# Attention scores for eight batches of eight heads: pairs of adjacent heads in block-diagonal q weights, and a new order of rows in the loads

## The chip, the cores and the metric

The kernel runs on one core of one Trainium2 chip. The metric is the device time of one execution in microseconds (us), as the median of several runs; lower is better.

## The reference

```python
batch, heads, seq, dim = 8, 8, 512, 64        # q, k: float32

def reference(q, k):
    scale = 1.0 / np.sqrt(q.shape[-1])
    return (np.einsum('bhqd,bhkd->bhqk', q, k) * scale).astype(np.float32)
```

For each of the 64 pairs of batch and head, a 512 x 64 matrix q is multiplied with the transpose of a 512 x 64 matrix k, and the result, 512 x 512, is scaled by 1/8. The inputs are 16.8 MB together and the output is 67.1 MB, all float32.

## The kernel before

The batches are taken two at a time: a unit v is batches 2v and 2v+1, and there are four units. A contraction over dim = 64 fills only half of the 128 rows of TensorE's array, so the two batches of a unit lie side by side: rows 0 to 63 hold the first batch, rows 64 to 127 the second (index x in the code).

**Loading and casting** (`load_and_cast`). For each unit and each of k and q, two loads (L70), one per batch, bring 1 MB each into a buffer `xf` of 128 partitions by 2048 floats. The view `q_r = q.rearrange("b g (m j) d -> b (g m) (j d)", j=R)` has R = 32: partition p is head g = p // 16 and row group m = p % 16, and it holds 32 consecutive rows of 64 floats, 8 KB. The source of one load is thus 1 MB of consecutive memory. A cast (L75) to bfloat16 follows, into half x of the tile `xb`; for unit 0 the casts are on VectorE and ScalarE, for the others on GpSimd (POOL). Six `xf` buffers and three `xb` buffers rotate.

**Transposing** (`transpose`). TensorE transposes 128 x 128 pieces of `xb`, 32 for k (L86) and 32 for q (L93) per unit, eight to a PSUM tile `tp` (two buffers). VectorE copies k's tiles into `kT` (L88), ScalarE q's into `qT` (L95). Afterwards partitions are (x, d), and the rows of a head are reached by strides. Each unit has its own `kT` and `qT`.

**Scores** (`scores`). One call works on two heads (2n and 2n+1) of both batches. Query row 8u + i of a head is row u of the stationary operand for that i. For each i there are four matmuls of 64 x 64 weights by 512 columns (L109), one for each head h and batch x. Their `tile_position=(x * D, h * U)` puts them on the four quarters of the array. Two values of i make one PSUM tile `ps` per batch, 128 x 1024 floats. It is scaled and copied to the output buffer `o`, alternately by ScalarE (L57) and VectorE (L59). When a buffer's four parts are filled, one transfer of 2 MB (L117) writes it to consecutive memory. Four `o` buffers rotate, and a call uses two of them.

**Order.** All transfers are issued by SyncE (SP), from one queue in program order, so the 16 loads stand ahead of the 32 outputs. A tile framework schedules the instructions of each engine by priority in program order and inserts the semaphores. By hand, the transposes of unit 1 stand behind the first call of `scores`, those of units 2 and 3 behind the second, so all transposes are done early. The rest of the scores follows.

Of the kernel before, what the change touches and what calls it, by code (L numbers as in the profile page):

```python
# [1 line left out]

# [5 lines left out]


@with_exitstack  # L10
def kernel(
    ctx: ExitStack,
    tc: tile.TileContext,
    q: bass.AP,
    k: bass.AP,
    out: bass.AP,
):

    nc = tc.nc
    B, H, S, D = q.shape
    scale = 1.0 / (D ** 0.5)
    P = 128
    UNITS = B // 2
    G = H
    M = P // G
    R = S // M  # L30
    RO = 8
    U = S // RO
    JJ = R // RO
    IW = 8 // JJ

    f32 = mybir.dt.float32
    bf16 = mybir.dt.bfloat16

    q_r = q.rearrange("b g (m j) d -> b (g m) (j d)", j=R)
    k_r = k.rearrange("b g (m j) d -> b (g m) (j d)", j=R)  # L40
    out_r = out.rearrange("b (n h) (u i) k -> b n (h u) (i k)", h=2, i=RO)

    consts = ctx.enter_context(tc.tile_pool(name="consts", bufs=1))
    raw_pool = ctx.enter_context(tc.tile_pool(name="raw", bufs=6))
    bf_pool = ctx.enter_context(tc.tile_pool(name="bf", bufs=3))
    t_pool = ctx.enter_context(tc.tile_pool(name="t", bufs=UNITS))
    out_pool = ctx.enter_context(tc.tile_pool(name="out", bufs=4))
    tpsum_pool = ctx.enter_context(tc.tile_pool(name="tpsum", bufs=2, space=bass.MemoryType.PSUM))
    psum_pool = ctx.enter_context(tc.tile_pool(name="psum", bufs=3, space=bass.MemoryType.PSUM))

    identity = None
    n_evac = 0

    def evacuate(dst, src):
        nonlocal n_evac
        if n_evac % 2 == 0:
            nc.scalar.mul(out=dst, in_=src, mul=scale)  # L57
        else:
            nc.vector.tensor_scalar(out=dst, in0=src, scalar1=scale, scalar2=None,  # L59
                                    op0=mybir.AluOpType.mult)  # L60
        n_evac += 1

    def load_and_cast(v):

        both = []
        for src in (k_r, q_r):
            xb = bf_pool.tile([P, R, 2, D], bf16, name="xb")
            for x in range(2):
                xf = raw_pool.tile([P, R * D], f32, name="xf")
                nc.sync.dma_start(out=xf, in_=src[2 * v + x])  # L70
                if v > 0:
                    copy = nc.gpsimd.tensor_copy
                else:
                    copy = (nc.vector.tensor_copy, nc.scalar.copy)[x]
                copy(out=xb[:, :, x, :], in_=xf.rearrange("p (j d) -> p j d", j=R))  # L75
            both.append(xb)
        return both

    def transpose(kb, qb):

        kT = t_pool.tile([P, P, R], bf16, name="kT")
        qT = t_pool.tile([P, RO, P, JJ], bf16, name="qT")
        for j0 in range(0, R, 8):
            tp = tpsum_pool.tile([P, 8, P], bf16, name="tp")
            for j in range(8):
                nc.tensor.transpose(out=tp[:, j, :], identity=identity,  # L86
                                    in_=kb[:, j0 + j].rearrange("p x d -> p (x d)"))
            nc.vector.tensor_copy(out=kT[:, :, j0:j0 + 8], in_=tp.rearrange("d j p -> d p j"))  # L88
        for i0 in range(0, RO, IW):
            tp = tpsum_pool.tile([P, IW, JJ, P], bf16, name="tp")  # L90
            for i in range(IW):
                for jj in range(JJ):
                    nc.tensor.transpose(out=tp[:, i, jj, :], identity=identity,  # L93
                                        in_=qb[:, RO * jj + i0 + i].rearrange("p x d -> p (x d)"))
            nc.scalar.copy(out=qT[:, i0:i0 + IW], in_=tp.rearrange("d i jj p -> d i p jj"))  # L95
        return kT, qT

    def scores(v, n, kT, qT):

        kTh = kT.rearrange("d (g m) j -> d g (m j)", g=G)  # L100
        qTh = qT.rearrange("d i (g m) jj -> d i g (m jj)", g=G)
        os = [out_pool.tile([P, RO, S], f32, name="o") for _ in range(2)]
        for i in range(0, RO, 2):
            pss = [psum_pool.tile([P, 2, S], f32, name="ps") for _ in range(2)]
            for w in range(2):
                for h in range(2):
                    for x in range(2):
                        rows = slice(x * D, (x + 1) * D)
                        nc.tensor.matmul(out=pss[x][h * U:(h + 1) * U, w, :],  # L109
                                         lhsT=qTh[rows, i + w, 2 * n + h, :],  # L110
                                         rhs=kTh[rows, 2 * n + h, :],
                                         start=True, stop=True,
                                         tile_position=(x * D, h * U))
            for x in range(2):
                evacuate(os[x][:, i:i + 2, :], pss[x])
        for x in range(2):
            nc.sync.dma_start(out=out_r[2 * v + x, n], in_=os[x].rearrange("p i k -> p (i k)"))  # L117

    cast = [load_and_cast(0)]
    identity = consts.tile([P, P], dtype=bf16)  # L120
    make_identity(nc, identity)
    for v in range(1, UNITS):
        cast.append(load_and_cast(v))

    ts = [transpose(*cast[0])]
    scores(0, 0, *ts[0])
    ts.append(transpose(*cast[1]))
    scores(0, 1, *ts[0])
    ts.append(transpose(*cast[2]))
    ts.append(transpose(*cast[3]))  # L130
    for v in range(UNITS):
        for n in range(2 if v == 0 else 0, H // 2):
            scores(v, n, *ts[v])


# [1 line left out]
_INS = ['q', 'k']  # L137
_OUTS = [((8, 8, 512, 512), 'float32')]


# [23 lines left out]
```

## Time and profile before

| | |
|---|---|
| median of 3 runs | 204.52 us (204.51 to 207.3) |
| profiled execution, its own time | 204.67 us |
| span of its profile | 202.9 us |
| TensorE (matmuls) busy | 134.3 us (66%) |
| VectorE busy | 96.2 us (47%) |
| ScalarE busy | 84.1 us (41%) |
| GpSimd (POOL) busy | 23.4 us (12%) |
| share of the 16 DMA engines' time, main queue | 97.6% |
| chain of work that ended last: DMA | 61% of the span |

The span runs from the first to the last recorded instruction; the execution's own time has a little more around it. An engine's busy time is the sum of its instructions' durations. The line of 40 slices gives one digit per slice of 5.07 us, the busy share in tenths; the GB/s line gives what the DMA engines moved in each. In the list of groups a row gives the line of the code, the engine, the operation, its output and input tiles with their sizes, the count, the total busy time and the mean of one, and then the idle time just before these instructions with what ended most of it.

### The profile page before, as it was taken

What the parts mean: (1) busy time and instruction counts of PE and PEld (TensorE: products, weight loads), DVE (VectorE), ACT (ScalarE), POOL (GpSimd) and SP (SyncE); (2) the same over time, 40 slices, a digit from 0 to 9 for tenths busy, and PEclk for the clock granted to TensorE, in tenths of its full rate; (3) what the DMA queues carried; (4) which work ended last, traced back from release to release, by engine and by line L of the source; (5) the groups of instructions that cost most, each with busy time, mean ns of one, the idle gap of its engine ahead of it and who ended that gap; (6) DMA issues with size and microseconds to landing.
All of it is one profiled execution on the core that took longest, in us unless ns stands there. A gap on an engine that the chain in (4) does not pass through costs nothing.

```text
span 202.9 us, 1888 instructions
## 1 busy us (share of the span) xinstructions
PE 134.3 (66%) x768; PEld 40.9 (20%) x768; DVE 96.2 (47%) x82; ACT 84.1 (41%) x83; POOL 23.4 (12%) x18
## 2 busy tenths in 40 slices
PE   0079698666396968787878787877778696766000
PEld 0066245454021111120211021111111121110000
DVE  0292799935182726354453636271809090909000
ACT  2336849265725243443525252535352525252000
POOL 1007757753000000000000000000000000000000
PEclk9999999999755555555555555555555555555555
DMA  5999999999999999999999999999999999999991
GB/s 218 431 426 423 418 426 417 420 428 423 439 423 426 436 430 430 433 426 433 426 426 433 428 428 430 436 423 426 433 423 436 431 423 436 426 423 433 433 426 74
DMA packets 6921, 84.01 MB, mean 414 GB/s; under 512 B 768, under 2 KB 768, under 8 KB 768
## 3 DMA queue, kind: packets, MB, share of 16 engines
q1 hardware_dynamic: 6912, 83.89, 97.6%
q8 instruction: 6, 0.10, 0.2%
q14 instruction: 3, 0.02, 0.0%
HBM read 16.78 MB, written 67.11 MB: 413 GB/s over the span
## 4 chain that ended last, share of the span: by engine, by line
DMA 61%; DVE 12%; PE 8%; ACT 7%; SPq 2%; issue 1%; DVEq 0%
DMA out_dram<-o 57%; DVE o L59 9%; PE ps L109 6%; ACT o L57 5%; DMA xf<-in_q_dram 4%; DVE kT L88 2%; ACT qT L95 2%; PE tp L93 2%; SPq L117 1%; PE tp L86 1%; DVE xb L75 1%; SPq L70 0%; DVEq L59 0%
## 5 line engine op out<-in xcount | busy, mean ns | idle before, releaser
L109 PE MATMUL ps<-kT,qT 64*64 64x512 bf16 x512 | 113.5, 584 | 35.2 <-ACT o L57 29.5
L59 DVE TENSOR_SCALAR o<-ps 128x1024 f32<-128x1024 f32 x64 | 75.6, 1220 | 78.5 <-DMA out_dram<-o 72.8
L57 ACT ACTIVATE o<-ps 128x1024 f32<-128x1024 f32 x64 | 63.9, 1024 | 82.9 <-PE ps L109 82.8
L109 PEld LDWEIGHTS <-qT 64*64 64x64 bf16 x512 | 23.2, 127 | 120.4 <-issue 117.8
L75 POOL CAST xb<-xf 128x2048 bf16<-128x2048 f32 x12 | 22.7, 1895 | 23.2 <-DMA xf<-in_k_dram 18.1
L88 DVE COPY kT<-tp 128x1024 bf16<-128x1024 bf16 x16 | 18.7, 1216 | 3.4 <-PE tp L86 3.3
L86 PE MATMUL tp<-identity,xb 128*128 128x128 bf16 x128 | 11.3, 241 | 13.2 <-ACT xb L75 10.1
L95 ACT COPY qT<-tp 128x1024 bf16<-128x1024 bf16 x16 | 15.6, 1016 | 10.3 <-PE tp L93 10.1
L93 PE MATMUL tp<-identity,xb 128*128 128x128 bf16 x128 | 10.7, 235 | 3.5 <-DVE kT L88 1.7
L86 PEld LDWEIGHTS <-xb 128*128 128x128 bf16 x128 | 9.0, 108 | 17.1 <-ACT xb L75 10.1
L93 PEld LDWEIGHTS <-xb 128*128 128x128 bf16 x128 | 8.7, 105 | 6.9 <-issue 5.7
L75 ACT CAST xb<-xf 128x2048 bf16<-128x2048 f32 x2 | 3.8, 1897 | 9.2 <-DMA xf<-in_k_dram 6.1
L75 DVE CAST xb<-xf 128x2048 bf16<-128x2048 f32 x2 | 2.5, 1228 | 9.4 <-DMA xf<-in_k_dram 5.6
L75 ACT ACT_TABLE_LOAD x1 | 1.3, 1283 | 0.7 <-PEq L148 0.7
masks.py:199 POOL TENSOR_SCALAR_AFFINE_SELECT identity<-identity 128x128 bf16<-128x128 bf16 x1 | 0.3, 293 | 0.1
masks.py:197 POOL MEMSET identity<- 128x128 bf16 x1 | 0.2, 205 | 0.3 <-POOLq L148 0.3
L148 POOL MEMSET const-float32-0.0<- 128x1 f32 x1 | 0.1, 100 | 0.2 <-issue 0.2
L148 POOL MEMSET const-bfloat16-1.0<- 128x1 bf16 x1 | 0.1, 102 | 0.0
L148 POOL MEMSET const-uint8-127<- 128x1 uint8 x1 | 0.1, 102 | 0.0
L148 POOL MEMSET const-float32-1.0<- 128x1 f32 x1 | 0.1, 99 | 0.0
## 6 DMA issues: line engine op xcount, KB each, us to landing
out_dram<-o SPq DMA_DIRECT2D x32, 2048.0 KB, 14.4
xf<-in_k_dram SPq DMA_DIRECT2D x8, 1024.0 KB, 14.0
xf<-in_q_dram SPq DMA_DIRECT2D x8, 1024.0 KB, 13.7
```

The lines of the kernel that those rows point to most:

```text
L57: nc.scalar.mul(out=dst, in_=src, mul=scale)
L59: nc.vector.tensor_scalar(out=dst, in0=src, scalar1=scale, scalar2=None, op0=mybir.AluOpType.mult)
L75: copy(out=xb[:, :, x, :], in_=xf.rearrange("p (j d) -> p j d", j=R))
L86: nc.tensor.transpose(out=tp[:, j, :], identity=identity, in_=kb[:, j0 + j].rearrange("p x d -> p (x d)"))
L88: nc.vector.tensor_copy(out=kT[:, :, j0:j0 + 8], in_=tp.rearrange("d j p -> d p j"))
L93: nc.tensor.transpose(out=tp[:, i, jj, :], identity=identity, in_=qb[:, RO * jj + i0 + i].rearrange("p x d -> p (x d)"))
L95: nc.scalar.copy(out=qT[:, i0:i0 + IW], in_=tp.rearrange("d i jj p -> d i p jj"))
L109: nc.tensor.matmul(out=pss[x][h * U:(h + 1) * U, w, :], lhsT=qTh[rows, i + w, 2 * n + h, :], rhs=kTh[rows, 2 * n + h, :], start=True, stop ...
L117: nc.sync.dma_start(out=out_r[2 * v + x, n], in_=os[x].rearrange("p i k -> p (i k)"))
L148: nc = _bacc.Bacc("TRN2", target_bir_lowering=False, num_devices=1)
```

## The change

- **Units and halves.** A unit is still two batches, but the halves x are now the even and the odd heads: half x of pair (b, n) is head 2n + x of batch b. There are eight pairs c = (b, n) in a unit.
- **Loads.** One load takes all even or all odd heads of both batches: `src[v, x]` has 16 row groups m, then 8 pairs c, then 8 KB. Partition p is m = p // 8 and pair c = p % 8. The source of one load is 128 pieces of 8 KB. Two that follow one another in one row group m lie 256 KB apart.
- **Weights.** q is kept in two standing tiles `qz`, used in turn by the units. For each i and pair c, `qz` holds 128 x 128 weights: rows 0 to 63 and columns 0 to 63 are the even head's q, rows 64 to 127 and columns 64 to 127 the odd head's. The other two quarters are zero; `clear` (L82) writes them once at the start, one of the four by VectorE and three by GpSimd. Copies of q (L105) touch only the two filled quarters, one half on VectorE and the other on ScalarE.
- **Matmuls.** One matmul of 128 x 128 weights by 512 columns (L116) gives 64 query rows of both heads, so there are 256 in place of 512. An output buffer holds one pair of heads.
- **Copies of k** (L94) alternate between VectorE and ScalarE, and lay `kT` out by pair.
- **Order.** The transposes of unit v + 1 stand in the middle of the scores of unit v.
- **Buffers.** `xf` 6 to 4, `xb` 3 to 5, `kT` 4 to 2, `o` 4 to 5.

In the changed kernel the transposes are L91 and L100, and the output transfer is L120; L57, L59, L70 and L75 keep their numbers.

```diff
-    G = H
-    M = P // G
+    C = H
+    M = P // C
...
-    q_r = q.rearrange("b g (m j) d -> b (g m) (j d)", j=R)
-    k_r = k.rearrange("b g (m j) d -> b (g m) (j d)", j=R)
-    out_r = out.rearrange("b (n h) (u i) k -> b n (h u) (i k)", h=2, i=RO)
+    q_r = q.rearrange("(v b) (n x) (m j) d -> v x m (b n) (j d)", b=2, x=2, j=R)
+    k_r = k.rearrange("(v b) (n x) (m j) d -> v x m (b n) (j d)", b=2, x=2, j=R)
+    out_r = out.rearrange("(v b) (n x) (u i) k -> v (b n) (x u) (i k)", b=2, x=2, i=RO)
...
-    raw_pool = ctx.enter_context(tc.tile_pool(name="raw", bufs=6))
-    bf_pool = ctx.enter_context(tc.tile_pool(name="bf", bufs=3))
-    t_pool = ctx.enter_context(tc.tile_pool(name="t", bufs=UNITS))
-    out_pool = ctx.enter_context(tc.tile_pool(name="out", bufs=4))
+    raw_pool = ctx.enter_context(tc.tile_pool(name="raw", bufs=4))
+    bf_pool = ctx.enter_context(tc.tile_pool(name="bf", bufs=5))
+    t_pool = ctx.enter_context(tc.tile_pool(name="t", bufs=2))
+    out_pool = ctx.enter_context(tc.tile_pool(name="out", bufs=5))
...
-                nc.sync.dma_start(out=xf, in_=src[2 * v + x])
+                nc.sync.dma_start(out=xf, in_=src[v, x])
...
+    def clear(engine, qz, x):
+
+        rows = slice(x * D, (x + 1) * D)
+        engine.memset(qz[rows, :, :, (1 - x) * U:(2 - x) * U], 0.0)
+
+    def transpose(v, kb, qb):
...
-        kT = t_pool.tile([P, P, R], bf16, name="kT")
-        qT = t_pool.tile([P, RO, P, JJ], bf16, name="qT")
-        for j0 in range(0, R, 8):
+        kT = t_pool.tile([P, C, M, R], bf16, name="kT")
+        qz = qzs[v % 2]
+        for n, j0 in enumerate(range(0, R, 8)):
...
-            nc.vector.tensor_copy(out=kT[:, :, j0:j0 + 8], in_=tp.rearrange("d j p -> d p j"))
+            copy = (nc.vector.tensor_copy, nc.scalar.copy)[n % 2]
+            copy(out=kT[:, :, :, j0:j0 + 8].rearrange("d c m j -> d m c j"),
+                 in_=tp.rearrange("d j (m c) -> d m c j", c=C))
...
-            nc.scalar.copy(out=qT[:, i0:i0 + IW], in_=tp.rearrange("d i jj p -> d i p jj"))
-        return kT, qT
+            for x in range(2):
+                rows = slice(x * D, (x + 1) * D)
+                copy = (nc.vector.tensor_copy, nc.scalar.copy)[x]
+                copy(out=qz[rows, i0:i0 + IW, :, x * U:(x + 1) * U]
+                     .rearrange("d i c (m jj) -> d i c m jj", jj=JJ),
+                     in_=tp[rows].rearrange("d i jj (m c) -> d i c m jj", c=C))
+        return kT, qz
...
+                nc.tensor.matmul(out=ps[:, w, :], lhsT=qz[:, i + w, c, :],
+                                 rhs=kT[:, c].rearrange("d m j -> d (m j)"),
+                                 start=True, stop=True)
+            evacuate(o[:, i:i + 2, :], ps)
+        nc.sync.dma_start(out=out_r[v, c], in_=o.rearrange("p i k -> p (i k)"))
...
+    qzs = [consts.tile([P, RO, C, P], bf16, name=f"qz{n}") for n in range(2)]
+    clear(nc.vector, qzs[0], 0)
+    clear(nc.gpsimd, qzs[0], 1)
+    for x in range(2):
+        clear(nc.gpsimd, qzs[1], x)
...
-    ts = [transpose(*cast[0])]
-    scores(0, 0, *ts[0])
-    ts.append(transpose(*cast[1]))
-    scores(0, 1, *ts[0])
-    ts.append(transpose(*cast[2]))
-    ts.append(transpose(*cast[3]))
+    ts = {0: transpose(0, *cast[0])}
...
-        for n in range(2 if v == 0 else 0, H // 2):
-            scores(v, n, *ts[v])
+        for c in range(C):
+            scores(v, c, *ts[v])
+            if c == C // 2 - 1 and v + 1 < UNITS:
+                ts[v + 1] = transpose(v + 1, *cast[v + 1])
```

More of the change, by code (lines that the diff above doesn't have):

```diff
@@ L37 @@
     bf16 = mybir.dt.bfloat16
-    q_r = q.rearrange("b g (m j) d -> b (g m) (j d)", j=R)
-    k_r = k.rearrange("b g (m j) d -> b (g m) (j d)", j=R)
-    out_r = out.rearrange("b (n h) (u i) k -> b n (h u) (i k)", h=2, i=RO)
+    q_r = q.rearrange("(v b) (n x) (m j) d -> v x m (b n) (j d)", b=2, x=2, j=R)
+    k_r = k.rearrange("(v b) (n x) (m j) d -> v x m (b n) (j d)", b=2, x=2, j=R)
+    out_r = out.rearrange("(v b) (n x) (u i) k -> v (b n) (x u) (i k)", b=2, x=2, i=RO)
     consts = ctx.enter_context(tc.tile_pool(name="consts", bufs=1))
-    raw_pool = ctx.enter_context(tc.tile_pool(name="raw", bufs=6))
-    bf_pool = ctx.enter_context(tc.tile_pool(name="bf", bufs=3))
-    t_pool = ctx.enter_context(tc.tile_pool(name="t", bufs=UNITS))
-    out_pool = ctx.enter_context(tc.tile_pool(name="out", bufs=4))
+    raw_pool = ctx.enter_context(tc.tile_pool(name="raw", bufs=4))
+    bf_pool = ctx.enter_context(tc.tile_pool(name="bf", bufs=5))
+    t_pool = ctx.enter_context(tc.tile_pool(name="t", bufs=2))
+    out_pool = ctx.enter_context(tc.tile_pool(name="out", bufs=5))
     tpsum_pool = ctx.enter_context(tc.tile_pool(name="tpsum", bufs=2, space=bass.MemoryType.PSUM))
     psum_pool = ctx.enter_context(tc.tile_pool(name="psum", bufs=3, space=bass.MemoryType.PSUM))
-    identity = None
     n_evac = 0
@@ L77, in load_and_cast @@
         return both
-    def transpose(kb, qb):
-        kT = t_pool.tile([P, P, R], bf16, name="kT")
-        qT = t_pool.tile([P, RO, P, JJ], bf16, name="qT")
-        for j0 in range(0, R, 8):
+    def clear(engine, qz, x):
[5 more added lines that the diff above has]
+        for n, j0 in enumerate(range(0, R, 8)):
             tp = tpsum_pool.tile([P, 8, P], bf16, name="tp")
@@ L94, in transpose, with scores @@
                                         in_=qb[:, RO * jj + i0 + i].rearrange("p x d -> p (x d)"))
-            nc.scalar.copy(out=qT[:, i0:i0 + IW], in_=tp.rearrange("d i jj p -> d i p jj"))
-        return kT, qT
[L98 to L102, printed above, removed]
+            for x in range(2):
[5 more added lines that the diff above has]
+        return kT, qz
+    def scores(v, c, kT, qz):
+        o = out_pool.tile([P, RO, S], f32, name="o")
         for i in range(0, RO, 2):
-            pss = [psum_pool.tile([P, 2, S], f32, name="ps") for _ in range(2)]
+            ps = psum_pool.tile([P, 2, S], f32, name="ps")
             for w in range(2):
[L106 to L117, printed above, removed]
+                nc.tensor.matmul(out=ps[:, w, :], lhsT=qz[:, i + w, c, :],
[3 more added lines that the diff above has]
+        nc.sync.dma_start(out=out_r[v, c], in_=o.rearrange("p i k -> p (i k)"))
     cast = [load_and_cast(0)]
```

## The prediction

> **What bounds the kernel now.** I read the slices and the queue totals first, then the stages, then who waits at the outputs, then the load stage in order of time.
>
> ```profile
> DMA  5999999999999999999999999999999999999991
> GB/s 218 431 426 423 418 426 417 420 428 423 439 423 426 436 430 430 433 426 433 426 426 433 428 428 430 436 423 426 433 423 436 431 423 436 426 423 433 433 426 74
> ...
> q1 hardware_dynamic: 6912, 83.89, 97.6%
> ...
> HBM read 16.78 MB, written 67.11 MB: 413 GB/s over the span
> ```
>
> From the second slice to the last but one the 16 DMA engines are full, and no slice moves more than 439 GB/s. The stages say the same:
>
> ```profile
> core 0: us, PE busy (x) PEld busy (x) DVE busy (x) ACT busy (x) POOL busy (x), PEclk, DMA share, GB/s
> ...
> 3.00:43.00 40.00, 26.37 (x268) 16.63 (x269) 25.61 (x22) 22.26 (x22) 19.86 (x11) 1.00 1.01 423
> ...
> 60.00:180.00 120.00, 92.91 (x397) 18.55 (x392) 56.55 (x48) 49.48 (x50) 0.00 (x0) 0.50 1.01 429
> ```
>
> The first row is the loads, the second the outputs. Both have a DMA share of 1, at 423 and 429 GB/s. In the output stage TensorE runs at half clock and VectorE and ScalarE are under half busy. The waits of VectorE and the chain of waits confirm that compute waits for DMA:
>
> ```profile
> DVE o L59 <- DMA out_dram<-o: 72.8, 14, 6.8
> ...
> 69.84 14.39 DMA out_dram<-o
> ...
> 89.29 14.39 DMA out_dram<-o
> ```
>
> The chain repeats every 89.29 - 69.84 = 19.45 us, which is one turn of the four output buffers: 4 x 2.097 MB / 19.45 us = 431 GB/s, or 4.86 us an output. The load stage, by the casts, each of which starts when its load has landed:
>
> ```profile
> 5.62 1.23 DVE L75 CAST xb<-xf 128x2048 bf16<-128x2048 f32 x1 [5.62 <-DMA xf<-in_k_dram]
> ...
> 10.59 1.23 DVE L75 CAST xb<-xf 128x2048 bf16<-128x2048 f32 x1 [3.74 <-DMA xf<-in_q_dram]
> ...
> 15.59 1.89 POOL L75 CAST xb<-xf 128x2048 bf16<-128x2048 f32 x1 [14.28 <-DMA xf<-in_k_dram]
> ```
>
> Loads 0, 2 and 4 land 4.98 us apart: 2.49 us a load of 1.049 MB, 421 GB/s. So the span is made of 16 x 2.49 = 39.8 us of loads, 32 x 4.86 = 155.5 us of outputs, and 202.9 - 195.3 = 7.6 us of start and tail. The profiled execution took 204.67 us, 1.77 us more than its span, and the median of the runs is 204.52; I forecast the median, as 204.52 plus what the span changes.
>
> [...]
>
> **The change, part by part.**
>
> Loads (L70). There are still 16 of 1.049 MB, in rows of 8 KB. Before, the source of one is 128 rows in sequence, a slowest dimension of 128 on both sides. After, it is 16 row groups (m) by 8 heads (b n), the SBUF side still 128 partitions. [...] a load goes at half rate: 16 x 2.49 = 39.8 us more. [...] I take a small lead, f = 0.2, my choice: 39.8 x 1.8 = 71.7 us, 31.9 more. Bounds: 0 (the order of rows still spreads, or the leads drift apart) and 39.8. A gain is excluded above about 1 us[...]. Nothing hides a slow load: all 16 loads stand ahead of the first output in SP's queue (before and after, by the order of SP's instructions), and the transfers are the path.
>
> Raw buffers, 6 to 4. Load i+4 waits for cast i, which starts as load i lands; with 2.49 us a load three more are then in flight, 7.5 us of transfer, against a cast of at most 1.9 us. Cost 0; if the cover were gone, one cast a load, 1.9 us.
>
> Clears (L82). VectorE's lies before its first cast. On POOL, 128 columns of MEMSET take 205 ns and one column 100, so 0.83 ns an element: 4096 elements are 3.4 us, and three of them end near 11 us, before POOL's first cast at 15.59. Lower bound 0. Upper bound: [...] rows might cost twice the estimate; POOL then starts its casts some 6 us late, loads wait as long, and the span takes up to 6 us.
>
> Transposes and copies. kT copies (L94) go half to each of VectorE and ScalarE, 2 x 1.22 and 2 x 1.02 us per unit; the q copies (L105) become 4 + 4 half-height ones of the same 1024 elements, which I take at 1.22 and 1.02 (from L88 and L95; the height should not shorten them[...]). Per unit VectorE has 16 x 1.22 + 6 x 1.22 = 26.8 us and ScalarE 16 x 1.02 + 6 x 1.02 = 22.4, against the 8 x 4.86 = 38.9 us that a unit's outputs take to leave. Cost 0.
>
> Matmuls (L116). 512 of 64 x 64 become 256 of 128 x 128, all 512 columns wide. [...] At half clock 427 ns each[...], 8 x 0.427 = 3.4 us an output against 4.86. A unit adds 64 transposes; in groups of 8 they took 0.62 us at full clock, so 10 us a unit at half: 27 + 10 = 37 of 38.9 us. This is tight, but five output buffers hold 24 us of transfers, and TensorE ran at 1.00 in the stage where it was kept busy. Cost 0; upper bound a few us.
>
> Outputs (L120). Same 2 MB blocks of contiguous memory, one buffer at a time, five instead of four. The queue stays full. Cost 0.
>
> Sum: 31.9 us, so 204.52 + 31.9 = 236.4 us.
>
> **Rivals.** (1) The loads keep their rate[...]. For it: [...] everything else is hidden under a full DMA queue. [...] Its price is 0 and it decides when f is near 1: 204.5 us, no change. This is the case on the other side of mine. (2) Leads drift and settle half way, f about 0.65: 39.8 x 0.35 = 13.9, so 218.4 us. [...] (3) Rates hold, but POOL's clears delay the casts: up to 6 us, 210.5 us. Against it: POOL idles until 15.59 now. (4) The jumps between rows of 256 KB in memory slow the reads themselves: the same sign and, at half rate, 244 us.
>
> **How the numbers follow.** Pairs near step 0.53, partial 0.19, clears 0.04, memory 0.03; loads unharmed 0.19; a gain of over 2% 0.02, since 7.6 us of start and tail is all that full DMA engines leave. Two per cent, about what a measurement of this kernel can tell from no change, is 4.1 us: slower 0.79, same 0.19, faster 0.02. My case alone gives 222 to 245 us. To hold 8 in 10 the range must reach down to the unharmed loads: 204 to 245.
>
> **What would show it.** In the profile after, casts of the load stage would be 4.5 us apart, the GB/s line would read 220 to 260 for the first 75 us with the DMA share still near full (packets of a load taking about twice as long), and then 430 for 156 us; the first output would start near 65 us, not 32. Casts 2.49 us apart would prove me wrong at once. Gaps in the DMA share during loads with POOL's clears or casts in them would be rival 3; low DMA share in the output stage with TensorE full would mean that the matmuls' doubling decides, which I cost at nothing.

## The result and the profile after

The changed kernel takes 240.4 us (median of 4 runs, 239.46 to 241.31), the kernel before 204.66: a ratio of 1.171, interval 1.161 to 1.182. It is 35.7 us slower. The profiled execution took 240.3 us with a span of 238.5.

The slices and the queue of the changed kernel; a slice is now 5.96 us:

```profile
DMA  6999999999999999999999999999999999999993
GB/s 150 220 220 218 221 214 225 216 224 220 220 220 224 385 434 434 431 431 423 429 433 431 435 423 426 437 426 437 429 423 440 425 431 431 426 434 429 437 437 135
...
q1 hardware_dynamic: 6912, 83.89, 98.3%
```

The DMA engines look as busy as before, with as many packets and bytes. But for the first 78 us they move 220 GB/s while "busy", then 430 as before. Busy time of a DMA engine counts the time that its packets take, and those of the loads take twice as long (615 ns for 309, below). The stages of the changed kernel (length, the engines' busy time and instruction counts, TensorE's clock, DMA share, GB/s):

```profile
core 0: us, PE busy (x) PEld busy (x) DVE busy (x) ACT busy (x) POOL busy (x), PEclk, DMA share, GB/s
...
3.00:43.00 40.00, 16.66 (x116) 11.36 (x118) 17.78 (x15) 17.61 (x16) 15.41 (x7) 0.96 1.02 222
43.00:78.00 35.00, 10.59 (x71) 5.85 (x73) 10.64 (x10) 7.92 (x8) 14.94 (x8) 0.73 1.01 221
...
82.00:200.00 118.00, 69.45 (x293) 28.38 (x298) 70.61 (x59) 57.60 (x60) 0.06 (x1) 0.81 1.01 430
```

The casts of the load stage, by the instructions of VectorE and POOL in order of time, say how far apart loads land:

```profile
8.19 1.23 DVE L75 CAST xb<-xf 128x2048 bf16<-128x2048 f32 x1 [5.19 <-DMA xf<-in_k_dram]
17.74 1.23 DVE L75 CAST xb<-xf 128x2048 bf16<-128x2048 f32 x1 [8.33 <-DMA xf<-in_q_dram]
```
```profile
27.41 1.89 POOL L75 CAST xb<-xf 128x2048 bf16<-128x2048 f32 x1 [14.55 <-DMA xf<-in_k_dram]
```

Loads 0, 2 and 4 land 9.55 and 9.67 us apart: 4.81 us a load, against 2.49 before. Sixteen loads take 76.9 us instead of 39.8. The outputs stand behind all of them in SP's queue. SP's instructions, first of the kernel before and then of the changed one, show that the first output is issued at 64.55 us instead of 31.88, right behind the last load; by the slices, 430 GB/s are reached only when the loads have landed, near 78 us:

```profile
31.88 5.10 SPq L117 DMA_DIRECT2D out_dram<-o  x4
```
```profile
59.25 5.21 SPq L70 DMA_DIRECT2D xf<-in_q_dram  x2
64.55 24.26 SPq L120 DMA_DIRECT2D out_dram<-o  x6
```

In the trace's records of single packets, the median 8 KB packet of a load takes 615 ns instead of 309. The 16 KB packets of the outputs take 611 ns in both kernels. The same records hold 4-byte packets, one for each engine of a transfer, at the end of its rows (16 for each load here; 8 for each load of e5 and 4 for each quarter of a load in e8 below, where the DMA share is 0.50 and 0.25). In the changed kernel the 16 ends of a load lie within 0.62 us for the first seven loads, at 4.78 us a load: the engines are near step. From the eighth load on one of them is some 1.4 us behind the others.

### The profile page after: what moved, and what is told of

Read it like the earlier page. It is cut to its first block, busy times and chain, and to the rows that moved or that the text cites. A ratio compares the mean times of both kernels' runs of the same rounds, so it can differ in the third digit from the quotient of the medians.

```text
span 238.5 us, 1454 instructions
## 1 busy us (share of the span) xinstructions
PE 105.3 (44%) x504; PEld 48.3 (20%) x512; DVE 109.4 (46%) x91; ACT 90.8 (38%) x91; POOL 34.9 (15%) x21
## 3 DMA queue, kind: packets, MB, share of 16 engines
HBM read 16.78 MB, written 67.11 MB: 352 GB/s over the span
## 4 chain that ended last, share of the span: by engine, by line
DMA 68%; DVE 9%; PE 4%; ACT 3%; issue 3%; POOL 2%; SPq 1%; ACTq 0%; POOLq 0%
DMA out_dram<-o 47%; DMA xf<-in_q_dram 22%; DVE o L59 5%; PE ps L116 4%; ACT o L57 3%; POOL xb L75 2%; DVE qz L105 2%; DVE kT L94 1%; SPq L70 1%; DVE xb L75 1%; SPq L120 0%; PE tp L91 0%; ACTq L57 0%; POOLq L75 0%
## 5 line engine op out<-in xcount | busy, mean ns | idle before, releaser
L116 PE MATMUL ps<-kT,qz 128*128 128x512 bf16 x248 | 85.5, 475 | 73.5 <-ACT o L57 67.4
L59 DVE TENSOR_SCALAR o<-ps 128x1024 f32<-128x1024 f32 x64 | 78.2, 1222 | 83.4 <-DMA out_dram<-o 60.9
L57 ACT ACTIVATE o<-ps 128x1024 f32<-128x1024 f32 x64 | 62.4, 1022 | 94.9 <-DMA out_dram<-o 82.6
L116 PEld LDWEIGHTS <-qz 128*128 128x128 bf16 x256 | 28.5, 114 | 122.0 <-issue 109.6
L75 POOL CAST xb<-xf 128x2048 bf16<-128x2048 f32 x12 | 22.7, 1893 | 46.5 <-DMA xf<-in_k_dram 28.6
L91 PE MATMUL tp<-identity,xb 128*128 128x128 bf16 x128 | 12.8, 256 | 22.6 <-ACT xb L75 14.9
L105 DVE COPY qz<-tp 64x1024 bf16<-64x1024 bf16 x16 | 19.0, 1209 | 5.0 <-PE tp L100 5.0
L105 ACT COPY qz<-tp 64x1024 bf16<-64x1024 bf16 x16 | 16.0, 1007 | 5.9 <-DVE qz L105 5.3
L100 PE MATMUL tp<-identity,xb 128*128 128x128 bf16 x128 | 11.8, 247 | 13.7 <-ACT qz L105 5.8
L91 PEld LDWEIGHTS <-xb 128*128 128x128 bf16 x128 | 10.7, 118 | 26.3 <-ACT xb L75 14.9
L100 PEld LDWEIGHTS <-xb 128*128 128x128 bf16 x128 | 10.0, 113 | 18.0 <-issue 9.9
L94 DVE COPY kT<-tp 128x1024 bf16<-128x1024 bf16 x8 | 9.8, 1220 | 3.9 <-PE tp L91 3.9
L82 POOL MEMSET qz<- 64x4096 bf16 x3 | 11.5, 3830 | 0.1
L94 ACT COPY kT<-tp 128x1024 bf16<-128x1024 bf16 x8 | 8.1, 1013 | 7.4 <-PE tp L91 7.3
L75 ACT CAST xb<-xf 128x2048 bf16<-128x2048 f32 x2 | 3.8, 1897 | 15.6 <-DMA xf<-in_k_dram 10.9
L75 DVE CAST xb<-xf 128x2048 bf16<-128x2048 f32 x2 | 2.5, 1228 | 13.5 <-DMA xf<-in_q_dram 8.3
L82 DVE MEMSET qz<- 64x2048 uint32 x1 | 1.8, 1765 | 1.2 <-PEq L153 1.2
```

The lines of the kernel that those rows point to most:

```text
L82: engine.memset(qz[rows, :, :, (1 - x) * U:(2 - x) * U], 0.0)
L91: nc.tensor.transpose(out=tp[:, j, :], identity=identity, in_=kb[:, j0 + j].rearrange("p x d -> p (x d)"))
L94: copy(out=kT[:, :, :, j0:j0 + 8].rearrange("d c m j -> d m c j"), in_=tp.rearrange("d j (m c) -> d m c j", c=C))
L105: copy(out=qz[rows, i0:i0 + IW, :, x * U:(x + 1) * U] .rearrange("d i c (m jj) -> d i c m jj", jj=JJ), in_=tp[rows].rearrange("d i jj (m c ...
L116: nc.tensor.matmul(out=ps[:, w, :], lhsT=qz[:, i + w, c, :], rhs=kT[:, c].rearrange("d m j -> d (m j)"), start=True, stop=True)
```

## Experiments

Theory P: in the form of the load with 16 groups by 8 rows, DMA engines that are in step hinder one another, so the form alone makes the loads slow. In the expectations, f is the lead of one engine over another, as a share of four rows of 8 KB. Theory M: the jumps of 256 KB between rows slow the reads. Theory R: another part of the change takes some of the time. In e1 to e5 the rows come to other partitions than the scores assume, so their output is not the reference's; counts and sizes stay.

**One part undone: the load views alone (e1), and that part alone in the kernel before (e2).**

```diff
 e1: the changed kernel with
+    q_r = q.rearrange("b g (m j) d -> b (g m) (j d)", j=R)      # k_r likewise
...
+                nc.sync.dma_start(out=xf, in_=src[2 * v + x])
 e2: the kernel before with
+    q_r = q.rearrange("(v b) (n x) (m j) d -> v x m (b n) (j d)", b=2, x=2, j=R)      # k_r likewise
...
+                nc.sync.dma_start(out=xf, in_=src[v, x])
```

> The changed kernel with the load views of the kernel before: a load is 128 consecutive rows of 8 KB. The rows of the inputs come to other partitions than the scores assume, so heads are mixed; every count, size and wait stays. Theory P[...]: the load form alone costs the 35 us, so about 205 us, casts 2.49 us apart, load packets 309 ns. Theory R (something else of the change, such as doubled matmul columns, clears or buffers, takes part of it): the load stage returns to 421 GB/s but the total stays clearly above 205 us. Theory M (the 256 KB jumps in memory slow the reads): about 205 us too.

> The kernel before with the load views of the changed kernel and nothing else; partitions then hold other heads than the scores assume, all counts and sizes stay. Theory P: the load form alone makes it 34 us slower: about 239 us, casts 4.8 us apart, load packets 615 ns. Theory R: clearly less than 239 us, the difference being the share of the rest of the change.

e1 took 203.89 us (11 runs), a ratio of 0.996 (0.995 to 0.997) to the kernel before. e2 took 239.15 us (4 runs), a ratio of 1.169 (1.159 to 1.178). The load form alone makes the loss, and the rest of the change, by e1, saves about 0.8 us instead of costing. (Between e2 and the changed kernel the rest shows nothing: 239.15 and 240.4 us lie within each other's spread.) Theory R is out. The load stage of e1, by its stages:

```profile
3.00:43.00 40.00, 23.74 (x180) 15.38 (x181) 32.23 (x24) 25.21 (x24) 29.65 (x15) 1.00 1.02 422
```

and the slices of e2, the kernel before in all but the load views:

```profile
GB/s 159 222 228 222 224 229 222 229 221 225 221 228 236 433 433 420 431 436 433 425 425 439 428 431 418 440 436 431 420 431 439 431 420 432 436 431 414 433 439 105
```

**Form without jumps (e3), jumps without the form (e4).**

```diff
 e3: 16 groups by 8 rows, the rows of a group consecutive
+    q_r = q.rearrange("(v b) g (m j) d -> v (b g m) (j d)", b=2, j=R).rearrange("v (m x c) f -> v x m c f", m=M, x=2)      # k_r likewise
 e4: 128 rows in one dimension, 64 KB apart
+    q_r = q.rearrange("b g (m j) d -> (b g m) (j d)", j=R).rearrange("(p s) f -> s p f", s=8)      # k_r likewise
...
+                nc.sync.dma_start(out=xf, in_=src[2 * v + x])
```

> The changed kernel with loads in the same form of 16 groups by 8 rows, but the 8 rows of a group consecutive in memory (64 KB in one piece) and the groups 128 KB apart; heads are mixed, all counts and sizes stay. Theory P: the form decides, so nothing changes: load packets about 615 ns, 220 GB/s, casts 4.8 us apart, about 240 us. Theory M: without the 256 KB jumps from row to row the loads run at about 421 GB/s, packets 309 ns, about 205 us.

> The changed kernel with loads of 128 rows in one dimension, each row 64 KB after the one before, so that every row is a jump and rows four apart are 256 KB apart; heads are mixed, all counts and sizes stay. Theory P: 128 is the slowest dimension on both sides[...], load packets about 309 ns, about 205 us. Theory M: jumps at every row slow it at least as much as in the changed kernel: packets 600 ns or more, 240 us or more.

e3 took 237.96 us, e4 203.83 us, one run each, as for the runs below except the last. The slices of e3, then those of e4:

```profile
GB/s 150 223 230 226 225 230 225 232 223 232 229 228 248 432 436 425 433 427 430 433 426 433 429 427 430 433 433 430 430 427 432 430 430 433 430 427 433 430 433 130
```
```profile
GB/s 243 427 425 417 430 422 415 417 409 431 418 441 435 418 431 438 425 417 444 430 425 435 428 425 438 431 425 438 431 423 431 435 425 425 435 428 435 431 428 120
```

Without the jumps the loads are as slow (228 GB/s); with a jump at every row, but 128 rows in one dimension, they are fast (about 420). Theory M is out: in these arrangements it hardly matters where a row lies in memory (228 against 221 GB/s); it matters how the transfer's dimensions are written.

**Half as many engines (e5).**

```diff
+    q_r = q.rearrange("(v b) (n x) (m j) d -> v x (b n) m (j d)", b=2, x=2, j=R)      # k_r likewise
```

> The changed kernel with the two row dimensions of a load swapped: 8 pairs of heads by 16 row groups, the latter consecutive in memory; partitions then hold other rows than the scores assume, all counts and sizes stay. [...] Theory P: [...]packets still about 615 ns, about 108 GB/s, casts near 9.7 us apart, 16.78 MB in 155 us, total near 318 us. If only the number of engines counts: packets 309 ns, half of 421 GB/s, total near 244 us.

It took 261.78 us: neither number. The stages of e5 show why:

```profile
4.00:14.00 10.00, 0.00 (x0) 0.00 (x0) 1.23 (x1) 0.00 (x0) 7.76 (x4) 1.00 0.50 121
14.00:24.00 10.00, 1.26 (x13) 1.27 (x14) 0.00 (x0) 1.90 (x1) 0.00 (x0) 1.00 0.50 125
24.00:34.00 10.00, 2.49 (x22) 2.06 (x20) 3.58 (x3) 1.01 (x1) 0.00 (x0) 1.00 0.51 138
...
44.00:54.00 10.00, 4.12 (x21) 1.96 (x20) 3.16 (x4) 3.99 (x4) 3.79 (x2) 0.81 0.51 173
54.00:64.00 10.00, 6.55 (x45) 3.80 (x44) 6.64 (x6) 5.75 (x6) 3.79 (x2) 0.84 0.50 196
64.00:74.00 10.00, 8.01 (x46) 4.04 (x45) 7.71 (x7) 5.90 (x6) 3.79 (x2) 0.84 0.50 212
```

The DMA share stays at 0.50, which is 8 of 16 engines always busy. But the rate climbs from 121 GB/s, near half of the changed kernel's 220, to 212, half of the 421 of the kernel before; the median packet falls from 552 ns in the first of these stretches to 309 in the last. In the first load five of the eight engines end together; in the tenth, three end together and three others 1.11 us later. The same transfers, on as many engines, are first slow and later at full rate, while the engines' relative position changes: by theory P, they drifted here until nothing was in the way. Why the changed kernel's own loads do not drift free (214 to 225 GB/s in all of its load slices but the first) was not shown.

**The same form on four engines at a time (e8).**

```diff
-                nc.sync.dma_start(out=xf, in_=src[v, x])
+                for g in range(4):
+                    nc.sync.dma_start(out=xf[32 * g:32 * g + 32], in_=src[v, x, 4 * g:4 * g + 4])
```

> The changed kernel with each load cut into four of 32 partitions (4 row groups by 8 heads each, in the same places of memory and SBUF, same rows of 8 KB, same 256 KB jumps). [...] Theory P: packets 309 ns, about 106 GB/s, 158 us for the loads, total near 322 us. If this form of load is slow by itself[...]: packets 615 ns, 53 GB/s, total near 480 us.

It took 319.94 us, and the median packet of a load 309 ns. Its slices, 7.95 us each:

```profile
DMA  1222222222222222228999989999999999999951
GB/s 68 106 107 106 107 107 107 109 104 106 107 107 106 105 106 107 107 106 343 417 433 416 425 375 398 428 430 427 431 431 427 429 429 431 425 429 425 425 229 84
```

A quarter of the engines moves 107 GB/s, half of what 16 engines do in the changed kernel, with the same rows, places and jumps. That is 27 GB/s for each of the four, against 421 / 16 = 26 in the kernel before. This form of load is not slow by itself; it is slow when other engines work beside it.

**Leads made on purpose (four runs).** Two transfers into an unread tile go ahead of the loads, of 16 and 48 rows. Their 4-byte packets show 4 and 12 engines, not which, so four rows for each; by the plan the 4 are among the 12, and the engines start the loads at three different times. W is 1024, 2048, 4096 or 5632 floats (rows of 4, 8, 16 or 22 KB, a nominal lead of 2, 4, 8 or 11 rows of 8 KB); there are four output buffers, three in the last run, whose `rows` are cut from a shorter piece of k.

```diff
+    lead = consts.tile([64, W], f32, name="lead")
+    rows = k.rearrange("b h s d -> (b h s d)").rearrange("(a r f) -> a r f", f=W, r=8)
+    nc.sync.dma_start(out=lead[48:64], in_=rows[0:4, 0:4])
+    nc.sync.dma_start(out=lead[0:48], in_=rows[0:12, 0:4])
     cast = [load_and_cast(0)]
```

> As the run with a lead of four rows, with rows of 4 KB in the two extra transfers, so the lead is two rows of 8 KB, f = 0.5. Theory P with preserved leads: [...]281 GB/s in the load stage, 60 us for the loads, about 226 us. [...]

> The changed kernel with two small transfers ahead of the loads into a tile that nobody reads (and four output buffers instead of five to make room)[...]. Theory P with preserved leads: f is 1[...], packets fall towards 309 ns and the load stage towards 421 GB/s; about 207 us with some 2.5 us for the extra transfers. If leads vanish[...]: packets 615 ns, 242 us. If they drift: in between, the load stage slowing with time.

> As the run with a lead of four rows, with rows of 16 KB in the two extra transfers, so the lead is eight rows[...]. Theory P with preserved leads: the pairs are in step again, one load apart, packets 615 ns, 220 GB/s, about 244 us. A theory in which any lead helps: about 209 us.

The three took 237.58, 235.06 and 217.67 us. The middle of the load stage in each, in that order:

```profile
5.00:74.00 69.00, 25.06 (x180) 16.48 (x183) 27.34 (x22) 23.58 (x22) 26.47 (x13) 0.83 1.01 235
```
```profile
5.00:72.00 67.00, 23.80 (x180) 15.77 (x183) 25.86 (x22) 23.58 (x22) 26.72 (x13) 0.85 1.02 248
```
```profile
8.00:56.00 48.00, 23.36 (x180) 15.98 (x183) 25.68 (x22) 23.59 (x22) 22.79 (x12) 0.93 1.01 352
```

A lead changes the rate, but none of my three numbers held: 4 nominal rows gave little, 8 gave most. SP's instructions in the third of these runs show one thing that I had left out:

```profile
0.74 0.84 SPq L124 DMA_DIRECT2D lead<-in_k_dram  x1
1.64 0.84 SPq L125 DMA_DIRECT2D lead<-in_k_dram  x1
```

The second transfer is issued 0.90 us after the first. From this and the time of an undisturbed row I reckoned a lead of 4 x 0.62 - 0.90 = 1.58 us for 8 nominal rows, and set a fourth run by it, with a lead of a whole load, eight rows:

> As the run with a nominal lead of eight rows, with rows of 22 KB in the two extra transfers (and three output buffers to make room). The trace of that run shows the two extra transfers issued 0.90 us apart, so the lead it really made was near 4 x 0.62 - 0.90 = 1.6 us, about the 1.24 us of four rows, and it moved 360 GB/s. Here the lead is near 4 x 0.85 - 0.90 = 2.5 us[...]. Theory P: in step again, load stage back at 220 to 260 GB/s, about 232 to 243 us. If a longer lead were merely better, or any disturbance helped: 360 GB/s or more, 219 us or less.

Its load stage:

```profile
12.00:80.00 68.00, 22.93 (x174) 16.02 (x175) 23.79 (x20) 21.56 (x20) 18.91 (x10) 0.82 1.01 235
```

235 GB/s: slow again with a longer lead, as theory P asks, and against "any disturbance helps". But the leads were not the reckoned ones, because the rows of the extra transfers were slow too: in the median 1.18 us for 16 KB and 1.62 us for 22 KB, against 0.62 and 0.85 in the reckoning. In the fourth run the extra transfers ended only at 14.6 us, where the reckoning has them end near 9; that more than covers the 0.8 us by which 243.8 us lies above the range I had given. The 4-byte packets, followed from the first load on, show the leads that were there once the loads ran evenly. The engines end a load in groups of four, eight and four, as the extra transfers divide them, here by the mean of each group:

| nominal rows | us a load | second group after the first, us | third after the second, us | in rows (a load is 8) |
|---|---|---|---|---|
| 2 | 4.47 | near 0 | 0.67 | 0 and 1.2 |
| 4 | 4.19 | 1.17 | 1.05 to 1.26 | 2.2 and 2.0 to 2.4 |
| 8 | 2.82 | 1.27 | 1.55 | 3.6 and 4.4 |
| 11 | 4.50 | 3.6 to 3.9 | 3.3 to 3.7 | 6.4 to 7.0 and 5.9 to 6.5 |

The fast run is the one in which the groups stand about four rows apart, half a load; near 0 and near 8 rows the loads are slow. With 4 nominal rows the lead in time was nearly the 1.24 us that I meant, but at 0.52 us a row it is only some two rows. So the rate went with the lead. A straight line between half rate in step (0 or 8 rows) and full rate at four rows, with the worse distance of each run, would give 211, 281, 383 and 241 GB/s (an estimate from this table and the 421 of the kernel before), where a load of 1.049 MB in the times above makes 235, 250, 372 and 233. The two faster runs come out in their order, and the size is only rough. Why a run has one rate although its two distances differ, as in the first of these runs, stays open.

**A mend that keeps the computation (e6).**

```diff
+    q_r = q.rearrange("(v b) (n x) (p j) d -> v x p (b n) (j d)", b=2, x=2, p=P)      # k_r likewise
...
+                nc.sync.dma_start(out=xf.rearrange("p (c f) -> p c f", c=C), in_=src[v, x])
...
+            copy(out=kT[:, j0 // 4:j0 // 4 + 2], in_=tp.rearrange("d (c j) p -> d c p j", j=4))
...
+                copy(out=qz[rows, :, c0:c0 + 2, x * U:(x + 1) * U].rearrange("d (w j) c u -> d c w j u", w=2),
+                     in_=tp[rows].rearrange("d c j (u w) -> d c w j u", w=2))
```

> The changed kernel with the whole computation kept and another deal of rows: partition p holds rows 4p to 4p+3 of each head, so a load is 128 partitions by 8 heads by 1 KB, with 128 the slowest dimension on both sides; the copies of transposed q and k are regrouped to fit (same counts and sizes). Theory P: the load stage returns to about 421 GB/s if pieces of 1 KB move as fast as rows of 8 KB, and the time to what the run with 128 consecutive rows gave, 203.9 us, which is below both kernels. If small pieces cost, the load stage is longer by that: at 10% slower loads 4 us more, 208 us. If the form of the load were not the cause: 240 us.

It took 212.36 us (5 runs), a ratio of 1.038 (1.036 to 1.039) to the kernel before. The load stage, by its stages, and the packets, from its page:

```profile
3.00:43.00 40.00, 24.07 (x180) 15.52 (x181) 29.52 (x24) 24.92 (x24) 24.90 (x12) 1.00 1.10 350
```
```profile
DMA packets 21255, 83.98 MB, mean 399 GB/s; under 512 B 768, under 2 KB 17152, under 8 KB 17152
```

The right form recovers 28 of the 35.7 us, but with pieces of 1 KB the loads run at 350 GB/s instead of 422, which is 16.78 / 0.350 - 16.78 / 0.422 = 8.2 us of the 8.5 that are left against e1. Whether it is the size of the pieces or the third dimension of the transfer was not tested apart. No kernel here that keeps the computation beats the kernel before.

## Why the prediction was right

**The bound.** It named the DMA engines as the bound, and loads and outputs as two stages that add up, because all loads stand ahead of the first output in SP's queue. After: 76.9 us of loads, then 430 GB/s.

**The mechanism.** From the trace alone nothing told how a load's rows are dealt to the engines. The step that carried the forecast, from the new form of the load to half the rate, was the author's estimate, and no trace of the kernel before shows it. e1 to e4 show that the form is the cause and memory is not: 422 and 419 GB/s in the load stages of e1 and e4, 225 and 228 in e2 and e3. e5, e8 and the leads speak for engines that hinder one another, by their relative position: 121 to 212 GB/s at 8 engines all the while in e5, packets of 309 ns with four engines at work in e8, and 352 GB/s with groups about four rows apart. What they hinder one another at was not shown, and no record here says which engine writes which partition. Nor is it shown why being near step costs nothing in the form before, where the 16 ends of a load lie within 0.51 us for the first nine loads too, in packets of 309 ns.

**The size.** The prediction took a load at 2 - f times its time before, the author's estimate, and the lead f = 0.2 was a choice and too large. A load took 4.81 / 2.49 = 1.93 times as long, so by the same reckoning f is 0.07, and the loads cost 37.1 us instead of 31.9. The upper bound, 39.8 us for half rate, was nearly met. The total came out closer, 240.4 against 236.4, in part because the rest of the change was forecast at 0 and is worth -0.8 us by e1. That much was luck.

**What was costed at nothing.** These lines of the changed kernel's page carry it:

```profile
L116 PE MATMUL ps<-kT,qz 128*128 128x512 bf16 x248 | 85.5, 475 | 73.5 <-ACT o L57 67.4
...
L105 DVE COPY qz<-tp 64x1024 bf16<-64x1024 bf16 x16 | 19.0, 1209 | 5.0 <-PE tp L100 5.0
L105 ACT COPY qz<-tp 64x1024 bf16<-64x1024 bf16 x16 | 16.0, 1007 | 5.9 <-DVE qz L105 5.3
...
L82 POOL MEMSET qz<- 64x4096 bf16 x3 | 11.5, 3830 | 0.1
```

The half-height copies take 1.21 and 1.01 us, as assumed. The clears take 3.83 us each on the mean, not 3.4 (3.51 the first, 8.04 the other two together, with a cast of VectorE among them), and end at 12.9 us, still before POOL's first cast at 27.41. TensorE was not at half clock in the output stage as I had reckoned but at 0.81 on the mean (matmuls of L116 in sequence start 427 ns apart in the median where the granted clock is 0.5, as reckoned, and 215 ns where it is 1), so the tight sum of 37 of 38.9 us never came up. DMA share stays at 1.01 there.

**The rivals.** Unharmed loads are excluded by the profile after, slow memory reads by e3 and e4. Drift to half way did not happen in the changed kernel, but it can't be ruled out for other loads: in e5 the rate climbed from 121 to 212 GB/s, half of the 421 of all 16 engines. The clears delayed no load.

## What to carry to other kernels

Before rearranging a DMA's source, write down its slowest dimension beside that of the SBUF side: here 16 groups by 8 rows moved 220 GB/s where 128 rows in one dimension moved 421, with the same engines, bytes, row sizes and a full DMA share. A full DMA share is no proof of full rate (1.02 at 222 GB/s in the changed kernel, 1.02 at 422 in e1); compare GB/s or the time of a packet between stages. In these DMA-bound stages the 128 x 128 matmuls and the added copies cost nothing (203.89 us in e1 against 204.67 for the kernel before, run beside it), and the one edit that looks like bookkeeping cost all of the 35.7 us.

## What the runs showed of the hardware beyond that

- Slow loads can become fast by themselves: 121 to 212 GB/s over some 60 us in e5, with no change in the form of the loads. In the changed kernel they did not (214 to 225).
- Small transfers ahead of slow loads can help much: with a lead of about four rows, the same loads ran at 352 GB/s instead of 221 on the mean, and the kernel took 217.67 us instead of 240.4.
- Rows 64 KB apart, all 128 of them, loaded as fast as consecutive ones (419 and 422 GB/s in the load stages of e4 and e1).
- A VectorE cast can take three times as long while POOL clears. In e1, where load 0 lands earlier than in the changed kernel, a cast within POOL's two later clears (4.83 to 12.86 us) took 3.80 us, hidden there by the loads in flight. In the changed kernel the cast at 8.19 us lies within the same clears (4.83 to 12.87 us) and took 1.23; what makes the difference was not shown. By VectorE's instructions of e1 in order of time:

```profile
5.62 3.80 DVE L75 CAST xb<-xf 128x2048 bf16<-128x2048 f32 x1 [2.62 <-DMA xf<-in_k_dram]
```
